# A two-layer encoder step on one core: first layer's 1/rms applied behind its projections, and a reordered recurrent branch

## The chip, the core and the metric

The kernel runs on one core of a Trainium2 chip. TensorE (PE) multiplies matrices into PSUM; VectorE (DVE), ScalarE (ACT) and GpSimd (POOL) do the elementwise work; SyncE (SP) issues all DMAs. The metric is the device time of one execution in microseconds (us), the median of a few executions. Times of single instructions, waits and clocks come from one profiled execution.

## What is computed

One inference step of a two-layer encoder, in fp32, for 1024 prompt frames and 64 sample frames (T = 1088 columns) of width 1024. Layer 0 (called AB in the kernel) feeds two attention groups from one projection; layer 1 (CD) feeds a forgetting attention C and a Griffin recurrent branch D. Around the change:

```python
def rmsnorm(x, g):
    y = x * lax.rsqrt(jnp.mean(x * x, axis=-1, keepdims=True) + EPS) * g

# each layer: x += W_out [mixer outputs](rmsnorm(x)); x += SwiGLU(rmsnorm(x))

def rg_lru(u, h0, w_a, b_a, w_x, b_x, lam):          # u: width-4 causal conv of dx
    r = sigmoid(blockdiag(u, w_a) + b_a)
    i = sigmoid(blockdiag(u, w_x) + b_x)
    log_a = -8.0 * r * softplus(-lam)
    a = exp(log_a)
    b = sqrt(-expm1(2.0 * log_a)) * (i * u)
    h = scan(a, b, h0)                                # h[t] = a[t] h[t-1] + b[t]
    # o_d = h * gelu(dg)
```

The projection of a normalized row is (x * g * 1/rms) W. Since 1/rms is one number per frame, it can be applied to x, or to the product (x * g) W.

## The kernel before, in words

Activations lie transposed: partitions are features (8 blocks k of 128), columns are frames, cut in three chunks `CH` of 384, 384 and 320 columns. Every fp32 matmul operand is split in a rounded high half and a remainder (`split`: ACT writes the high half, L235; DVE or POOL subtracts for the low half, L236), and a product takes three matmuls (high x high, high x low, low x high). A projection of one chunk by one weight block of 128 columns is therefore 8 x 3 = 24 matmuls (`gemm` L263 to L265; `gemm_steps` L275 where it is fed in slices between attention steps).

Layer AB consists of eight units, 0 to 7. A unit projects queries, keys and values (`proj`), unloads PSUM (`put_q`: ACT L351 and L352 write scaled high halves, DVE L356 the low halves; `new_k`: a DVE copy L369 to a staging tile, then `put_k` L332 to L335; `new_v`: DVE copy L379, PE transposes L385 and L388, then splits) and then computes scores (L487, L488), softmax and outputs, while the next unit's projections fill PE. Later units read the normalized halves `hh` and `hl` that unit 0 made.

`start` is unit 0. It loads x chunk 0 in eight pieces, then the query weights, then x chunk 1. `addsq` squares a piece on ACT (L300, L303) and adds on DVE (L304); `rms` averages by a matmul (L285) and takes 1/rms by Ln and Exp on ACT (L289 or L291, L292); `norm` multiplies x * g * r on DVE (L313) and splits the result. Chunk 0's norm comes first; its loop carries the squares of chunk 1. The key and value weights are loaded behind it. Then each chunk takes three projections; behind the query projection of a chunk stands the norm of the next one.

The order of each engine's instructions is laid out by a scheduler from data dependencies; `issue_after` keeps a named instruction ahead. Temporaries are rings: `tmp`, `stg` (staging, two slots), `nat`, `ot`; a ring's slot is reused when its last reader is done, a DMA that writes it out included. SP issues DMAs in order, and each waits for the one eight earlier.

At the head of layer CD, `recurrent` runs four blocks m = 0 to 3 of 128 features. For each it projects (`d_in`, `d_gate`: copy L1381), convolves on DVE (`d_conv` L1371, L1373), multiplies by the gate weights on PE (`d_gates` L1396 to L1398) with sigmoids on ACT (L1399) that free the PSUM banks, does gelu (`d_gelu`: ACT square L1355, POOL L1356, DVE L1357, ACT tanh L1360 and L1362, DVE L1363), and closes (`d_close`: POOL products L1411, ACT tanh L1413, exponentials and square roots L1418 to L1422, DVE scans L1425 and L1426). Between them `between` gives out six slices of C's first queries and keys. Sigmoid and tanh share one ACT table, the logarithm and exponential another; a change is a table load (L192). dx, u, G and R of a block are taken from a pool of eight slots and handed back by `d_close`, whose tile t overwrites u. DVE's forget-gate scans (L1306, L1307) stand between block 0 and 1.

## Time and profile before

| | us |
|---|---|
| median of 3 runs | 2711.04 |
| lowest, highest | 2710.79, 2717.03 |
| the profiled execution | 2712.83 |
| its span | 2711.0 |

The span of the profile is the time from the first to the last recorded instruction; the profiled execution's own time is 1.83 us more. A row of a timeline gives start, length, engine, line, operation, output<-input, and in brackets the idle time of the engine before it and what ended it. In the stretches (start:end, length, then busy time and number of instructions) a granted clock below 1.00 means that PE ran at a lower rate for part of the stretch. Of the page's parts, the busy times say which engine is the limit overall, the waits what PE stood still for, and the timeline where.

### The profile page before, as it was taken

The page shows a single profiled execution, that of the slowest core. Times are in us where ns is not written, and L with a number is a line of the kernel's source. Part 1 is how long each engine was busy: PE and PEld are TensorE (multiplying, and loading weights), DVE is VectorE, ACT ScalarE, POOL GpSimd, SP SyncE. Part 2 cuts the span into 40 slices and gives each one's busy share as a digit, 9 for nine tenths or more (in the row PEclk, how much of TensorE's full clock was granted, in tenths as well). Part 3 has the DMA queues.
Part 4 walks back from the last instruction along what each step waited for, and adds up shares of the span by engine and source line. Part 5 has one row for each costly group of instructions (what it writes and reads, how often), then busy time and mean ns, then how long its engine had stood idle before and what let it go on. Part 6 is the DMA issues. An engine that isn't in the chain of part 4 may idle for free. (4 is left out here: it accounts for less than half of the span.)

```text
span 2711.0 us, 44897 instructions
## 1 busy us (share of the span) xinstructions
PE 2596.9 (96%) x17610; PEld 2525.3 (93%) x17610; DVE 1325.7 (49%) x2763; ACT 1196.2 (44%) x2373; POOL 1155.1 (43%) x939
## 2 busy tenths in 40 slices
PE   6999999999999999999998979999999999999998
PEld 5899999889899999999998969988989999999998
DVE  7666666777432333422156557777743233242214
ACT  5666667764322233311135566686432323331112
POOL 5222222324666666422335433343366666641230
PEclk9999999999999999999999989999999999999999
DMA  6222222342222222442232342234322122244211
GB/s 204 73 71 69 78 63 62 104 151 92 83 95 66 81 72 87 141 154 72 74 105 60 52 80 79 78 123 150 100 86 97 64 82 70 88 141 153 72 55 67
DMA packets 115109, 250.21 MB, mean 92 GB/s; under 512 B 21432, under 2 KB 70848, under 8 KB 114896
## 3 DMA queue, kind: packets, MB, share of 16 engines
q1 hardware_dynamic: 114896, 247.33, 29.9%
q8 instruction: 138, 2.26, 0.4%
q14 instruction: 75, 0.61, 0.1%
HBM read 179.09 MB, written 65.43 MB: 90 GB/s over the span
## 5 line engine op out<-in xcount | busy, mean ns | idle before, releaser
L236 POOL TENSOR_TENSOR split_arena<-arena,split_arena 128x512 fp32r<-128x512 f32 (+5 forms) x501 | 756.7, 1522 | 1181.6 <-ACT split_arena L235 1091.7
L1070 PE MATMUL banks<-split_arena 128*128 128x272 f32 x7392 | 944.5, 290 | 23.3 <-ACT arena L1077 8.0
L1070 PEld LDWEIGHTS banks<-split_arena 128*128 128x128 f32 x7392 | 937.6, 190 | 30.0 <-ACT arena L1077 8.8
L235 ACT ACTIVATE split_arena<-arena 128x512 fp32r<-128x512 f32 (+10 forms) x664 | 458.8, 707 | 1020.3 <-PE banks L1070 291.9
L275 PE MATMUL banks<-split_arena 128*128 128x384 f32 (+1 forms) x3384 | 632.0, 333 | 3.4 <-POOL split_arena L236 2.3
L275 PEld LDWEIGHTS banks<-split_arena 128*128 128x128 f32 x3384 | 558.5, 189 | 10.9 <-POOL split_arena L236 2.9
L1182 PE MATMUL banks<-split_arena 128*128 128x384 f32 (+1 forms) x1056 | 345.1, 327 | 2.2 <-DVE arena L1148 1.4
L1184 PE MATMUL banks<-split_arena 128*128 128x384 f32 (+1 forms) x1056 | 344.4, 326 | 0.0
L1183 PE MATMUL banks<-split_arena 128*128 128x384 f32 (+1 forms) x1056 | 344.2, 326 | 0.0
L236 DVE TENSOR_TENSOR split_arena<-banks,split_arena 128x512 fp32r<-128x512 f32 (+4 forms) x312 | 167.4, 541 | 89.9 <-ACT split_arena L235 87.2
L499 DVE CUSTOM_DVE_ANT_0 arena<-banks,arena 128x384 f32<-128x384 f32 (+4 forms) x368 | 175.5, 493 | 56.4 <-PE banks L488 40.2
L1182 PEld LDWEIGHTS banks<-split_arena 128*128 128x128 f32 x1056 | 198.2, 188 | 3.6 <-DVE arena L1148 2.0
L1183 PEld LDWEIGHTS banks<-split_arena 128*128 128x128 f32 x1056 | 198.2, 188 | 0.3
L1184 PEld LDWEIGHTS banks<-split_arena 128*128 128x128 f32 x1056 | 198.2, 188 | 0.0
L235 ACT ACTIVATE split_arena<-banks 128x512 fp32r<-128x512 f32 (+4 forms) x312 | 146.7, 476 | 97.4 <-PE banks L604 43.3
L236 DVE TENSOR_TENSOR split_arena<-arena,split_arena 128x1088 fp32r<-128x1088 f32 (+8 forms) x163 | 154.0, 952 | 70.9 <-ACT split_arena L235 70.4
L1081 DVE TENSOR_TENSOR arena<-banks,arena 128x544 f32<-128x544 f32 (+1 forms) x46 | 32.2, 700 | 301.7 <-PE banks L1070 301.7
L501 ACT ACTIVATE arena<-arena 128x640 f32<-128x640 f32 (+8 forms) x216 | 156.3, 724 | 47.0 <-DVE arena L499 45.5
L1214 DVE TENSOR_TENSOR arena<-banks,arena 128x384 f32<-128x384 f32 (+1 forms) x96 | 51.1, 534 | 250.4 <-PE banks L1184 250.2
L604 PE MATMUL banks<-arena 128*128 128x128 f32 (+2 forms) x828 | 135.4, 276 | 18.8 <-DVE arena L520 11.5
L604 PEld LDWEIGHTS banks<-arena 128*128 128x128 f32 (+2 forms) x828 | 96.4, 141 | 37.7 <-DVE arena L520 15.1
L263 PE MATMUL banks<-split_arena 128*128 128x384 f32 (+1 forms) x312 | 106.7, 344 | 16.7 <-ACT arena L1399 10.0
(165 smaller groups left out, 3076.4 us busy)
## 6 DMA issues: line engine op xcount, KB each, us to landing
arena<-in_w_dram SPq DMA_DIRECT2D x120, 512.0 KB, 3.6
h_spill<-arena SPq DMA_DIRECT2D x22, 1088.0 KB, 4.2
arena<-h_spill SPq DMA_DIRECT2D x44, 544.0 KB, 4.4
arena<-in_abw_dram SPq DMA_DIRECT2D x24, 512.0 KB, 3.6
arena<-in_cdw_dram SPq DMA_DIRECT2D x20, 512.0 KB, 3.6
x_spill<-arena SPq DMA_DIRECT2D x48, 192.0 KB, 1.9
arena<-x_spill SPq DMA_DIRECT2D x16, 544.0 KB, 4.9
arena<-in_w_dram SPq DMA_DIRECT2D x19, 384.0 KB, 3.2
```

The source lines that it names most:

```text
L235: self.hi = self.nc.scalar.activation(hi, x, AF.Copy).ins
L236: lo = sub.tensor_tensor(lo, x, hi.bitcast(F32), op=ALU.subtract)
L263: nc.tensor.matmul(ps, wh[:, k], hh[k][:, c0:c0 + n], start=(k == ks[0]), stop=False)
L275: self.pe = self.nc.tensor.matmul(ps, x[:, k], y[k][:, c0:c0 + n], start=a and i == 0, stop=z and i == 2).ins
L499: nc.vector.tensor_tensor_reduce(o, p, t, -1.0, low, ALU.add, ALU.min, to)
L501: nc.scalar.activation(sb, sb, AF.Exp, bias=st[:, 0:1], scale=-1.0, accum_out=st[:, 1:2])
L604: nc.tensor.transpose(pt[:r, t * nq + s * m:t * nq + s * m + m], src, self.ident[:m, :m])
L1070: last = nc.tensor.matmul(bank[:, p], l[:, k], r[:, k, x], start=first and i == 0, stop=k == 3 and i == 2, skip_group_check=True)
L1182: nc.tensor.matmul(ps, wh, h[:, c0:c0 + n], start=j == j0, stop=False)
L1183: nc.tensor.matmul(ps, wh, lo[:, c0:c0 + n], start=False, stop=False)
L1184: nc.tensor.matmul(ps, wl, h[:, c0:c0 + n], start=False, stop=j == j1 - 1)
L1214: nc.vector.tensor_tensor(xs, pss[ci], xs, op=ALU.add)
```

## The change

Two independent parts. **First layer:** the high and low halves are made of x * g, without 1/rms. Query weights come first, then x chunk 0 in two halves of four pieces with the key weights between, then the value weights. The query and key projections of chunk 0 are each cut in two halves of k. The squares of a chunk stand behind its projections in the code, and 1/rms is kept in `self.rs` for all eight units and multiplied into the PSUM result: in place for queries, and as the unloading operation for keys and values. `norm` is not called by `start` any more; weights' low halves are made on DVE there. `layer_cd` sets `self.rs` to None.

**Recurrent branch:** the pool of slots is replaced by fixed places, with a place of its own for t; the tanh of gelu is held behind the sigmoids of the same block; the convolution of block m stands ahead of the closing of block m-1; the last slice of keys moves from the loop to behind the last gates.

```diff
+        self.rs = {c0: self.v(F_R + c0, n) for c0, n in CH}
...
     def put_q(self, d, c0, n, ps):
         nc = self.nc
+        if self.rs:
+            nc.vector.tensor_tensor(ps, ps, self.rs[c0], op=ALU.mult)
...
+    def unload(self, sg, c0, ps):
+
+        if self.rs:
+            self.nc.vector.tensor_tensor(sg, ps, self.rs[c0], op=ALU.mult)
+        else:
+            self.nc.vector.tensor_copy(sg, ps)
...
     def new_k(self, d, c0, n, ps, outs, keep, sub=None):
         sg = self.stg.get()[:, :n]
-        self.nc.vector.tensor_copy(sg, ps)
+        self.unload(sg, c0, ps)
+        if self.rs:
+            ps = sg
...
     def start(self, d, wq, wk, wv, pair, outs):
...
+        def parts(ci, ks=range(8)):
+
+            c0, n = CH[ci]
+            for k in ks:
+                x, g = self.x[k][ci], self.pcol(k)
+                hi, lo = self.hh[k][:, c0:c0 + n], self.hl[k][:, c0:c0 + n]
+                nc.scalar.activation(hi, x, AF.Copy, scale=g)
+                nc.vector.scalar_tensor_tensor(lo, x, g, hi.bitcast(F32), op0=ALU.mult, op1=ALU.subtract)
...
-        loadx(0)
-        w = [self.loadw(wq, rings)]
+        w = [self.loadw(wq, rings, sub=nc.vector)]
+        loadx(0, range(4))
+        parts(0, range(4))
+        w.append(self.loadw(wk, rings, sub=nc.vector))
+        loadx(0, range(4, 8))
+        parts(0, range(4, 8))
+        w.append(self.loadw(wv, rings, sub=nc.vector))
         loadx(1)
-        for k in range(8):
-            self.addsq(0, k, self.x[k][0])
-        last = self.norm(0, 0, 1, (nc.gpsimd, nc.gpsimd))
-        with self.tc.issue_after(last.ins):
-            w.append(self.loadw(wk, rings, sub=nc.vector))
-            w.append(self.loadw(wv, rings))
         loadx(2)
...
             p = [ring.get()[:, :n] for _ in range(3)]
-            for i in range(3):
+            if ci == 0:
+
+                for ks in (range(4), range(4, 8)):
+                    for i in range(2):
+                        for _ in self.gemm_steps(p[i], w[i], c0, n, ks=ks, first=ks[0] == 0, last=ks[0] == 4):
+                            pass
+            for i in range(2 if ci == 0 else 0, 3):
                 self.gemm(p[i], w[i], c0, n)
-                if i == 0 and ci < 2:
-                    self.norm(ci + 1, 0, 2 if ci == 0 else None)
+            for k in range(8):
+                self.addsq(ci, k, self.x[k][ci])
+            if ci < 2:
+                parts(ci + 1)
+            self.rms(ci, to=self.rs[c0], table=False)
             self.put_q(d, c0, n, p[0])
...
     def d_open(self, m, w=None):
-        b["slots"] = [self.D.get() for _ in range(3)]
-        for n, w, t in zip(("dx", "u", "G"), (T + 6, T + 6, T), b["slots"]):
-            b[n] = t[:, 0:w]
+        slot = lambda i, n: self.v(F_S + SLOT * i, n)
+        i, j, k, r = ((0, 1, 6, 4), (2, 3, 7, 4), (0, 1, 6, 7), (2, 3, 4, 1))[m]
+        b["dx"], b["u"], b["G"], b["R"], b["t"] = slot(i, T + 6), slot(j, T + 6), slot(k, T), slot(r, T), slot(5, T)
...
     def d_gelu(self, b, ci):
...
-        if ci == 0:
-            with self.tc.issue_after(self.table("sigmoid_and_others")):
-                nc.scalar.activation(z, z, AF.Tanh, scale=0.7978845608028654)
-        else:
-            nc.scalar.activation(z, z, AF.Tanh, scale=0.7978845608028654)
+        with self.tc.issue_after(b["gate"]):
+            b["tanh"] = nc.scalar.activation(z, z, AF.Tanh, scale=0.7978845608028654).ins
...
     def d_gates(self, b, m, after):
...
+        with contextlib.nullcontext() if self.closed is None else self.tc.issue_after(self.closed):
+            table = self.table("sigmoid_and_others")
...
-                nc.scalar.activation(dst[:, c0:c0 + n], ps, AF.Sigmoid, bias=self.dcol(bc, m))
+                with self.tc.issue_after(table):
+                    b["gate"] = nc.scalar.activation(dst[:, c0:c0 + n], ps, AF.Sigmoid, bias=self.dcol(bc, m)).ins
...
             self.d_gate(nb)
+            self.d_conv(nb, m)
             self.d_close(b, m - 1)
-            next(more)
-            self.d_conv(nb, m)
+            if m < 3:
+                next(more)
...
             self.d_gates(b, 3, b["pe"])
+            next(more)
             for ci in range(3):
                 self.d_gelu(b, ci)
```

How the order moves at three places. First ACT at the start of the program, before: L300 and L303 are the squares of x chunk 0, L235 128x1024 the high half of the query weights, L289 and L292 the Ln and Exp of 1/rms. (The brackets name the semaphores waited for: DMAHW is a load.)

```order
L300 ACTIVATE arena<-arena 128x384 [waits DMAHW1_49]
L303 ACTIVATE arena<-arena 128x384 [waits DMAHW2_49]
L303 ACTIVATE arena<-arena 128x384 [waits DMAHW3_49]
L303 ACTIVATE arena<-arena 128x384 [waits DMAHW4_49]
L303 ACTIVATE arena<-arena 128x384 [waits DMAHW5_49,DVE_49]
L303 ACTIVATE arena<-arena 128x384 [waits DMAHW6_49,DVE_49]
L303 ACTIVATE arena<-arena 128x384 [waits DMAHW7_49,DVE_49]
L303 ACTIVATE arena<-arena 128x384 [waits DMAHW0_49,DVE_49]
L192 ACT_TABLE_LOAD
L235 ACTIVATE split_arena<-arena 128x1024 [waits DMAHW1_49]
L300 ACTIVATE arena<-arena 128x384 [waits DMAHW2_49]
L289 ACTIVATE arena<-banks,arena 128x384 [waits PE_49]
```

The same place of the changed kernel, whose lines are its own: L224 128x1024 is the high half of weights, L449 that of x * g, L289 and L292 are now the squares.

```order
L224 ACTIVATE split_arena<-arena 128x1024 [waits DMAHW1_49]
L449 ACTIVATE split_arena<-arena 128x384 [waits DMAHW2_49]
L449 ACTIVATE split_arena<-arena 128x384 [waits DMAHW3_49]
L449 ACTIVATE split_arena<-arena 128x384 [waits DMAHW4_49]
L449 ACTIVATE split_arena<-arena 128x384 [waits DMAHW5_49]
L289 ACTIVATE arena<-arena 128x384
L292 ACTIVATE arena<-arena 128x384 x2
L224 ACTIVATE split_arena<-arena 128x1024 [waits DMAHW6_49]
L449 ACTIVATE split_arena<-arena 128x384 [waits DMAHW7_49]
```

The weights and the halves of x stand ahead of all squares. Further on, in the changed kernel, ACT comes to the last squares (L292 128x320) and the last 1/rms (L280, L281) in this order; L342 and L343 unload queries, L321 and L322 keys.

```order
L224 ACTIVATE split_arena<-arena 128x1024 [waits DMAHW7_49,PE_49]
L292 ACTIVATE arena<-arena 128x320 [waits DMAHW3_49,DVE_49]
L292 ACTIVATE arena<-arena 128x320 [waits DVE_49] x3
L280 ACTIVATE arena<-banks,arena 128x320 [waits PE_49]
L281 ACTIVATE arena<-arena 128x320 [waits Activation_49]
L342 ACTIVATE split_arena<-banks 64x320 [waits DVE_49]
L343 ACTIVATE split_arena<-banks 64x320
```

The first of these squares waits for a DMA, the one that writes chunk 1's new values out of a staging slot which overlaps the temporaries.

Second, ACT at the first block of the recurrent branch, before: L1355 is the square of gelu, L1360 and L1362 its tanh, L351 and L352 unload queries, L1399 are the sigmoids.

```order
L1355 ACTIVATE arena<-arena 128x384 [waits DVE_49]
L192 ACT_TABLE_LOAD
L1355 ACTIVATE arena<-arena 128x384 [waits Activation_49]
L1360 ACTIVATE arena<-arena 128x384 [waits DVE_49]
L351 ACTIVATE split_arena<-banks 64x384 [waits PE_49]
L352 ACTIVATE split_arena<-banks 64x384
L1399 ACTIVATE arena<-banks,arena 128x384 [waits PE_49] x2
```

In the changed kernel L1373 is that square, L342 and L343 unload queries, L181 is the table load, L1416 are the sigmoids, L1377 the tanh.

```order
L1373 ACTIVATE arena<-arena 128x384 [waits DVE_49]
L1373 ACTIVATE arena<-arena 128x384 [waits Activation_49]
L1373 ACTIVATE arena<-arena 128x320 [waits DVE_49]
L342 ACTIVATE split_arena<-banks 64x384 [waits PE_49]
L343 ACTIVATE split_arena<-banks 64x384
L181 ACT_TABLE_LOAD
L1416 ACTIVATE arena<-banks,arena 128x384 [waits PE_49] x2
```

The tanh moved behind the sigmoids, and the third square, which waits for DVE, ahead of them.

Third, PE at the gates of the last block, before: L1396 to L1398 are the gates' last matmuls, L487 and L488 the first scores of C, L275 the projection of values, L385 their transposes.

```order
L1396 MATMUL banks<-split_arena 128x320
L1397 MATMUL banks<-split_arena 128x320
L1398 MATMUL banks<-split_arena 128x320
L487 MATMUL banks<-split_arena 64x320
L488 MATMUL banks<-split_arena 64x320
L487 MATMUL banks<-split_arena 64x320
L275 MATMUL banks<-split_arena 128x384 x3
L275 MATMUL banks<-split_arena 128x320 x24
```

In the changed kernel L1412 to L1414 are the gates, L252 to L254 the last keys (20 of their 24 matmuls stand here, of which the first rows are shown).

```order
L1412 MATMUL banks<-split_arena 128x320
L1413 MATMUL banks<-split_arena 128x320
L1414 MATMUL banks<-split_arena 128x320
L253 MATMUL banks<-split_arena 128x320
L254 MATMUL banks<-split_arena 128x320
L252 MATMUL banks<-split_arena 128x320
```

The last keys moved from ahead of the gates to behind them; behind the 20 stand 35 matmuls of the value projection (L264) and then its first transposes (L385).

More of the change, by code (lines that the diff above doesn't have):

```diff
@@ L67 @@
 F_STG2 = 15808
+F_R = 14464
 GROUPS = [(12064 + 2176 * i, 544) for i in range(4)] + [(7360, 544), (38720, 544), (9536, 544), (4416, 544)] + \
@@ L115, in free @@
         del self.live[at]
-class Slots:
-    def __init__(self, ap, off, size, n):
-        self.all = [ap[:, off + size * i:off + size * (i + 1)] for i in range(n)]
-        self.free = list(self.all)
-    def get(self):
-        return self.free.pop(0)
-    def put(self, *slots):
-        self.free.extend(slots)
 class Blocks:
@@ L172, in __init__ @@
         self.tmp = self.tmp3
-        self.S, self.D = Heap(M, F_S, 6144), Slots(M, F_S, SLOT, 8)
+        self.S = Heap(M, F_S, 6144)
         self.stg, self.nat, self.ot = ring(F_STG, 384, 2), ring(F_NAT, 384, 2), ring(F_OT, 256, 2)
@@ L276, in gemm_steps, with rms @@
             yield "z", n * 1.25e-3
-    def rms(self, ci, parts=None, to=None):
+    def rms(self, ci, parts=None, to=None, table=True):
         nc = self.nc
@@ L286, in rms @@
         r = (self.rb.get() if to is None else to)[:, :n]
-        if ci == 0:
+        if ci == 0 and table:
             with self.tc.issue_after(self.table("natural_log_exp_and_others")):
@@ L378, in new_v @@
         sg = self.stg.get()[:, :n]
-        nc.vector.tensor_copy(sg, ps)
+        self.unload(sg, c0, ps)
         npr = min(n, TP - c0)
@@ L436, in start, with loadx @@
         ring = Ring(self.PS, [512 * i for i in range(5)], 512)
-        def loadx(ci):
+        def loadx(ci, ks=range(8)):
             c0, n = CH[ci]
-            for k in range(8):
+            for k in ks:
                 self.dma(self.x[k][ci], I["xT"][k * 128:k * 128 + 128, c0:c0 + n])
-        loadx(0)
-        w = [self.loadw(wq, rings)]
-        loadx(1)
-        for k in range(8):
-            self.addsq(0, k, self.x[k][0])
-        last = self.norm(0, 0, 1, (nc.gpsimd, nc.gpsimd))
-        with self.tc.issue_after(last.ins):
-            w.append(self.loadw(wk, rings, sub=nc.vector))
-            w.append(self.loadw(wv, rings))
+        def parts(ci, ks=range(8)):
+            c0, n = CH[ci]
+            for k in ks:
+                x, g = self.x[k][ci], self.pcol(k)
[9 more added lines that the diff above has]
+        w.append(self.loadw(wv, rings, sub=nc.vector))
+        loadx(1)
         loadx(2)
@@ L1405, in d_close @@
         c = self.rgc[:, m:m + 1]
-        t, a = u[:, 0:T], R
+        t, a = b["t"], R
         cuts = [slice(c0, c0 + n) for c0, n in CH]
@@ L1412, in d_close @@
         for x in cuts:
-            nc.scalar.activation(t[:, x], R[:, x], AF.Tanh, scale=c)
+            with self.tc.issue_after(b["tanh"]):
+                nc.scalar.activation(t[:, x], R[:, x], AF.Tanh, scale=c)
         table = self.table("natural_log_exp_and_others")
@@ L1421, in d_close @@
             nc.scalar.activation(t[:, x], t[:, x], AF.Ln, scale=-1.0)
-            nc.scalar.activation(t[:, x], t[:, x], AF.Exp, scale=0.5)
+            self.closed = nc.scalar.activation(t[:, x], t[:, x], AF.Exp, scale=0.5).ins
             nc.vector.tensor_tensor(Ig[:, x], Ig[:, x], t[:, x], op=ALU.mult)
@@ L1430, in d_close @@
         self.dma(self.oTd[4 + m], b["G"])
-        self.D.put(*b["slots"])
     def gate_weights(self):
@@ L1464, in recurrent @@
         self.gate_weights()
+        self.closed = None
         stg, self.stg2 = self.stg, Ring(self.M, [F_STG2], 384)
@@ L1516, in layer_cd @@
         self.lastu = 3
+        self.rs = None
         rest = self.recurrent(pending, self.qkv_views(0), W[0], W[4], I["cckT"][0], (O["c_kT"][0], O["sc_kT"][0]), 0)
```

5 lines of the change are left out of this document (1 added, 4 removed).

## The prediction

> **What bounds the kernel now.** I read the page first, then TensorE's (PE's) busy time by stretches, its waits, and its timeline where it waits.
>
> ```profile
> span 2711.0 us, 44897 instructions
> PE 2596.9 (96%) x17610; PEld 2525.3 (93%) x17610; DVE 1325.7 (49%) x2763; ACT 1196.2 (44%) x2373; POOL 1155.1 (43%) x939
> ```
>
> PE works 2596.9 of 2711.0 us. The change takes no matmul away, so it can win only PE's 114 us of idleness and the time PE runs at half rate. The stretches (start:end, length, PE busy, instructions, granted clock, DMA share, GB/s) say where those lie:
>
> ```profile
> 0.00:20.00 20.00, 4.16 (x8) 1.00 0.82 272
> 20.00:40.00 20.00, 17.07 (x75) 1.00 0.56 167
> 40.00:60.00 20.00, 16.32 (x80) 0.91 0.78 204
> 60.00:80.00 20.00, 16.59 (x89) 0.83 0.47 142
> 100.00:700.00 600.00, 579.88 (x3766) 550.65 (x3765) 408.31 (x1081) 390.40 (x867) 171.81 (x151) 0.99 0.27 82
> 1460.00:1480.00 20.00, 11.44 (x53) 0.74 0.39 113
> 1560.00:1580.00 20.00, 9.99 (x43) 0.74 0.42 14
> ```
>
> (In the 600 us row the busy times are PE, its weight loads, DVE, ACT, POOL.) Up to 80 us PE idles 25.9 us, two thirds of it in the first 20, where DMA is 82% busy. From 100 to 700 us it is 97% busy. In the recurrent section two stretches idle 8.6 and 10.0 us, at a clock of 0.74. PE's waits name the releasers (total, times, longest):
>
> ```profile
> PE banks L285 <- DVE arena L304: 12.8, 3, 11.1
> PE banks L263 <- ACT arena L1399: 10.0, 3, 8.6
> PE banks L487 <- POOL split_arena L334: 5.9, 1, 5.9
> PE banks L385 <- DVE arena L379: 5.8, 3, 3.7
> ```
>
> The first is the sum of squares ahead of the first projection; the second are the recurrent branch's sigmoids, which free PSUM banks; the third the last keys; the fourth transposes of values.
>
> **The start.** PE's own timeline (start, length; the bracket is the idle time before):
>
> ```profile
> 11.06 1.65 PE L285 MATMUL banks<-arena 128*128 128x384 f32 x2 [11.06 <-DVE arena L304]
> 16.82 0.69 PE L263 MATMUL banks<-split_arena 128*128 128x384 f32 x1 [4.11 <-ACT split_arena L235]
> 18.66 0.52 PE L265 MATMUL banks<-split_arena 128*128 128x384 f32 x1
> 18.98 0.52 PE L263 MATMUL banks<-split_arena 128*128 128x384 f32 x1
> 21.68 0.69 PE L264 MATMUL banks<-split_arena 128*128 128x384 f32 x1 [0.90 <-POOL split_arena L236]
> 26.94 0.34 PE L265 MATMUL banks<-split_arena 128*128 128x384 f32 x1
> 27.11 0.33 PE L263 MATMUL banks<-split_arena 128*128 128x384 f32 x1
> 74.04 0.31 PE L264 MATMUL banks<-split_arena 128*128 128x320 f32 x1
> 74.19 0.31 PE L265 MATMUL banks<-split_arena 128*128 128x320 f32 x1
> 76.53 0.33 PE L487 MATMUL banks<-split_arena 128*64 128x320 f32 x1 [2.03 <-issue]
> ```
>
> The first projection begins at 16.82, the first score at 76.53. Matmuls follow each other every 0.32 us at first (18.66 to 18.98), every 0.17 from about 27 on, every 0.15 when 320 wide. Three projections of three chunks are 72 matmuls a chunk: 144 x 0.173 + 72 x 0.147 = 35.5 us; with about 3.5 for the means (1.65 for the first two) and the transposes, 39. So 76.5 - 39 = 37.5 us before the first score are waits or half rate.
>
> What the pieces cost now:
>
> ```profile
> arena<-in_abw_dram SPq DMA_DIRECT2D x24, 512.0 KB, 3.6
> 11.72 1.06 ACT L235 ACTIVATE split_arena<-arena 128x1024 fp32r<-128x1024 f32 x1
> 21.97 1.21 DVE L236 TENSOR_TENSOR split_arena<-arena,split_arena 128x1024 fp32r<-128x1024 f32 x1
> 4.34 0.52 ACT L303 ACTIVATE arena<-arena 128x384 f32<-128x384 f32 x1
> 15.60 1.67 DVE L313 SCALAR_TENSOR_TENSOR arena<-arena 128x384 f32<-128x384 f32 x3
> 10.43 1.28 ACT L192 ACT_TABLE_LOAD   x1
> 16.84 4.79 POOL L236 TENSOR_TENSOR split_arena<-arena,split_arena 128x384 fp32r<-128x384 f32 x4 [1.58 <-ACT split_arena L235]
> 0.00:80.00 80.00, 45.17 (x93) 0.94 0.66 196
> ```
>
> After the change the query weights are issued first, at about 1.2: landed by 4.8 (3.6 us), high halves at 5.9 (ACT 1.06), then one high half of x (0.52). First matmul at about 6.6 instead of 16.8. Where it used to take a multiplication (DVE, 0.56), a rounding (ACT, 0.52) and a subtraction (POOL, 1.20) for each of 24 pieces of x, it takes the rounding and one DVE operation of 0.56. DVE then has 24 of these, 21 additions of the same size and three weight splits, 45 x 0.55 + 3 x 1.21 = 28 us by some 50: not the bound. PE's course: chunk 0 is 72 x 0.173 = 12.5, plus 4.0 for 27 matmuls at half rate (27 x 0.147), plus 1 for pieces that come late: done at about 24 (second half of x: 4 x 192 KB behind 1.8 MB, at 272 GB/s by 11 us, before PE has used the first). Chunk 1: 12.5 + 1.5, chunk 2: 10.6 + 1: done at 49.5.
>
> The sums of squares are late next. They no longer gate a projection, but each 1/rms gates unloading the chunk, and so the first score. ACT has 45.2 us of work in the first 80 (last row above, ACT alone) and about 43 still ahead of the first score; the squares share temporaries with the value copy and the cached keys, so two of them wait for value writes to land (192 KB, 2.8 us, behind 384 KB reads that take 6.6):
>
> ```profile
> rel_rows<-in_relrow_dram SPq DMA_DIRECT2D x8, 384.0 KB, 6.6
> out_a_vT_dram<-arena SPq DMA_DIRECT2D x2, 192.0 KB, 2.8
> ```
>
> I put the last 1/rms at 51.5 (50 to 58), and 5 us behind it, as now between copy, splits and score, the first score at 56.5 (54 to 62). By the new order 25 matmuls of the next unit (4.4 us) stand ahead of that score. So the waste is 56.5 - 39 - 4.4 = 13 instead of 37.5: a gain of 24. I take 22, since ACT at 43 of 56 us will be late somewhere; the range is 14 to 27.
>
> A rule speaks against this start. *TensorE: Matmul & The Clock Gate* of the Trainium skill (Part 1, HAM oscillation) says PE drops to half rate after an idle window of about 3.4 us, and that feeding it in pieces shorter than the waits keeps it there. The trace agrees after the 4.11 us wait (0.32 us a matmul until about 27); by the rule the sum above would hold only if the feed has no such gaps, and the third rival prices the contrary.
>
> **Multiplications by 1/rms.** Unit 0's nine are in the course above. Units 1 to 7 gain three each, 21 on DVE, in place in PSUM ahead of the query copy: as a 0.56 us operation each, 11.6 us. DVE is busy 68% from 100 to 700 us, PE 97%: they lie beside matmuls, and the copies of keys and values become multiplications of the same size. Their price is a bank freed 0.56 us later, against a chunk of 24 x 0.173 = 4.2 us: 0 to 3 us in all, I take 1. The table load that goes at the start (1.28 us of ACT) lies within the wait ahead of 16.82, which is counted whole above: 0 beyond it.
>
> **The recurrent section.**
>
> ```profile
> 1461.28 5.25 DVE L1306 TENSOR_TENSOR_SCAN arena<-arena 8x1024 f32<-8x1024 f32 x2 [2.39 <-DMA out_c_logfT_dram<-arena]
> 1469.73 1.01 DVE L1357 TENSOR_TENSOR arena<-arena 128x384 f32<-128x384 f32 x2
> 1472.38 0.69 PE L263 MATMUL banks<-split_arena 128*128 128x384 f32 x1 [8.56 <-ACT arena L1399]
> 1565.07 0.44 PE L1396 MATMUL banks<-split_arena 128*128 128x384 f32 x1 [3.27 <-ACT split_arena L235]
> 1566.33 0.69 PE L1397 MATMUL banks<-split_arena 128*128 128x384 f32 x1 [0.82 <-DVE split_arena L236]
> 1576.83 0.53 PE L487 MATMUL banks<-split_arena 128*64 128x320 f32 x1 [5.91 <-POOL split_arena L334]
> 1587.35 0.69 PE L385 MATMUL banks<-arena 128*128 128x128 f32 x2 [3.73 <-DVE arena L379]
> ```
>
> *First block, 8.56 us.* "Sigmoids ahead" does not cure it. In the new order all three gelu squares still precede the sigmoids on ACT, and the third needs a two-slot buffer that a DVE multiplication frees, which stands behind the forget-gate scans and two steps of the convolution (done 1469.7). The square then runs at about 1470.3, and the query copies and a table load of 1.28 before the sigmoids: the bank comes at 1473.6 instead of 1472.4, **1.2 us worse**.
>
> *Last block.* The convolution of m=3 goes ahead of the closing of m=2, so the gates' 3.27 + 0.82 and about 2 of half rate go (the clock of this stretch is 0.74): -6. The 20 matmuls left of the last keys and 24 of the values now stand behind the gates, in the 5.91 wait: -5.9. What is late next: the first transposes of values wait for a DVE copy behind the third gelu, at about 1578 to 1580, by which PE will have done 7 us of this work: 3 to 4 us come back, and another 1 to 2 at the out_c_vT buffer that DVE reaches earlier. Blocks two and three: 0 (the sigmoids' other two waits are 10.0 - 8.6 = 1.4 us together, and move either way). Sum 1.2 - 6 - 5.9 + 5 = **-6** (-9 to +1).
>
> **The sum.** -22 + 1 - 6 = -27, with the profiled execution's 2712.83 (span 2711.0 and 1.8 around it) 2685.8; it lies 1.8 above the median of 2711.04, so for the median 2711.0 - 27 = 2684.
>
> **Rivals.**
> 1. *The rms chain takes the gain.* Squares and 1/rms of chunk 2 come late (ACT's 43 us, value writes behind 384 KB reads): first score at 64 to 68. For it: ACT's load. Against: the squares have no other reader. The start gives 13 to 16, the rest as above or less: total -12 to -19, about 2696.
> 2. *Everything works.* First score at 53, DVE's copy no longer late: -27 and -9 to -11: about 2674.
> 3. *PE stays at half rate.* If waits for pieces of x, weights and DVE halves kept the first 216 matmuls slow, they cost 0.147 each for 189 more of them, 27.8 us: nothing is won, 2712. Against: the wait of 0.90 us at 21.68 did not keep PE from full rate by 27. This is what the page named above would expect of a starved start.
> 4. *Slower: the query multiplications hold banks.* A multiplication queued on DVE, in order, behind another unit's softmax holds its projection's bank. It decides once a chunk is held longer than the 4.2 us of matmuls that cover it by 1.7 us: 21 x 1.7 = 36 us against 27 won, 2720. For it: DVE at 68%. Against: keys and values already wait for such a DVE copy today, and from 100 to 700 us all waits of PE together are 3%.
> 5. *The start does not begin earlier*, because weights and x share DMA at 82% and land together: PE begins at 12, 5 us later than forecast, with the rest in step; -22 in all, inside the forecast's range.
>
> **The numbers.** The forecast (-20 to -33, rival 5 in it) 0.56; rival 1 (-9 to -20) 0.20; rival 2 (beyond -33) 0.14; rival 3 and its like, within 0.3% (8 us, about what a measurement of this kernel can tell from no change), 0.05; rival 4, 0.05. Faster 0.90. The range leaves out the ends of rivals 1 and 2 and both last ones: 2673 to 2698.
>
> **What would show it.** Right: first projection near 6.6, first score near 56, PE's first 80 us with 10 to 14 us less idle than 25.9 plus half-rate matmuls fewer; the 8.56 wait still there, near 9.8; the waits at 1565 and 1576 gone, one for the value copy left. Wrong: first score after 62 with ACT or a value write as releaser (rival 1); spacing of 0.32 beyond 20 us (rival 3); new waits of PE on the query multiplication between 100 and 1300 us (rival 4); a first block without a wait.

## The result, and the profile after

The change takes 2691.72 us (median of 4 runs, 2690.54 to 2694.74) against 2714.03 us for the kernel before beside it (four runs; the three with the median of 2711.04 are among them): a ratio of 0.9921, 95% interval 0.9907 to 0.9936, some 21 us (17 to 25). The same kernel, run again beside experiments on two later occasions, gave 0.9909 (0.9895 to 0.9922) and 0.9920 (0.9907 to 0.9934). The forecast was 27 us less, 2684, in a range of 2673 to 2698. The time lies 7.7 us above the forecast: the gain is 4.7 us smaller (22.3 by the medians), and the kernel before took 3 us more here than the 2711.04 that the forecast started from.

The page and PE's stretches of the change (start:end, length, PE busy, instructions, clock, DMA share, GB/s):

```profile
span 2690.5 us, 44858 instructions
PE 2592.6 (96%) x17610; PEld 2525.5 (94%) x17610; DVE 1320.8 (49%) x2781; ACT 1196.9 (44%) x2372; POOL 1133.1 (42%) x921
```

```profile
0.00:20.00 20.00, 12.51 (x56) 1.00 0.89 310
20.00:40.00 20.00, 20.00 (x118) 1.00 0.76 227
40.00:60.00 20.00, 14.60 (x83) 0.83 0.71 207
60.00:80.00 20.00, 19.88 (x120) 1.00 0.21 53
1440.00:1460.00 20.00, 9.90 (x51) 0.75 0.44 128
1520.00:1540.00 20.00, 15.83 (x80) 0.83 0.41 50
1560.00:1580.00 20.00, 14.30 (x73) 0.83 0.63 96
```

PE's busy time fell by 4 us (the count of matmuls is the same, and one at half rate counts longer), the span by 20.5. In the first 80 us PE idles 13.0 us where it idled 25.9. One stretch of the start is now bad (40 to 60), and the recurrent section has three. PE's largest waits:

```profile
PE banks L252 <- ACT arena L1416: 14.3, 2, 10.1
PE banks L385 <- DVE arena L354: 9.3, 2, 5.9
PE banks L274 <- DVE arena L293: 7.1, 3, 5.4
```

The sigmoids (L1416) head the list with more than before (10.0 then); the wait on the sum of squares (L293) is down from 12.8. The start on PE's, ACT's and DVE's timelines:

```profile
6.89 0.69 PE L264 MATMUL banks<-split_arena 128*128 128x384 f32 x1 [6.89 <-ACT split_arena L449]
...
22.81 0.81 PE L274 MATMUL banks<-arena 128*128 128x384 f32 x2
...
53.43 1.43 PE L274 MATMUL banks<-arena 128*128 128x320 f32 x2 [5.40 <-DVE arena L293]
54.19 4.52 PE L264 MATMUL banks<-split_arena 128*128 128x384 f32 x15
...
60.51 0.30 PE L504 MATMUL banks<-split_arena 128*64 128x320 f32 x1
```

```profile
47.67 0.47 ACT L292 ACTIVATE arena<-arena 128x320 f32<-128x320 f32 x1 [4.12 <-DMA out_a_vT_dram<-arena]
...
55.47 0.47 ACT L281 ACTIVATE arena<-arena 128x320 f32<-128x320 f32 x1
```

```profile
48.18 5.20 DVE L293 TENSOR_TENSOR arena<-arena 128x320 f32<-128x320 f32 x6 [6.07 <-ACT arena L292]
```

The first projection begins at 6.89 (forecast 6.6), chunk 0 is done at 22.8 (24), the first score comes at 60.5 (56.5, within 54 to 62). In between stands the wait that the forecast named: ACT stands 4.12 us until chunk 1's values are written out of the staging slot that its temporaries overlap, DVE adds late, PE waits 5.40 for the last mean, and 15 matmuls behind it take 4.52 us, about 0.3 each: half rate. The last 1/rms (L281) is ready at 55.9, 4.6 us ahead of the first score.

The recurrent section of the change, PE, then ACT and DVE:

```profile
1457.36 0.69 PE L252 MATMUL banks<-split_arena 128*128 128x384 f32 x1 [10.10 <-ACT arena L1416]
1533.28 0.69 PE L252 MATMUL banks<-split_arena 128*128 128x384 f32 x1 [4.17 <-ACT arena L1416]
1565.69 0.69 PE L385 MATMUL banks<-arena 128*128 128x128 f32 x2 [5.93 <-DVE arena L354]
```

```profile
1454.06 0.47 ACT L1373 ACTIVATE arena<-arena 128x320 f32<-128x320 f32 x1 [7.10 <-DVE arena L1375]
...
1527.92 0.47 ACT L1373 ACTIVATE arena<-arena 128x320 f32<-128x320 f32 x1 [4.40 <-DVE arena L1375]
```

```profile
1524.75 0.85 DVE L1386 TENSOR_SCALAR arena<-arena 128x1091 f32<-128x1091 f32 x1 [6.55 <-DMA arena<-in_dconvT_dram]
```

The third gelu square (L1373 128x320) waits 7.10 us for DVE, and six sigmoids wait behind it, as forecast. A second wait for sigmoids, of 4.17 us, was not forecast: in the third block the same square waits 4.40 us for DVE, and DVE for the input of the convolution (6.55, L1386).

Where the 20.5 us lie along the program is read from the first and last starts of lines that stand for places: unit 0's first outputs (L541, now L558), the feed-forward part (L1070, now L1087), the gates of the recurrent branch (L1396, now L1412) and the scores (L487, now L504). A row gives the shortest, median and longest duration in ns, then first and last start. Before, and then the change:

```profile
L541 PE MATMUL banks<-arena x40: 275/378/483, 96.9 to 322.6; 128*128 128x256 f32 x32, 128*128 128x64 f32 x8
L1070 PE MATMUL banks<-split_arena x7392: 282/288/595, 663.0 to 2436.9; 128*128 128x272 f32 x200
L1396 PE MATMUL banks<-split_arena x24: 306/337/522, 1460.7 to 1570.3; 128*128 128x384 f32 x16, 128*128 128x320 f32 x8
L487 PE MATMUL banks<-split_arena x312: 277/365/793, 76.5 to 1883.6; 128*128 128x384 f32 x68, 128*128 128x512 f32 x48, 128*128 128x256 f32 x28, 128*64 128x320 f32 x12
```

```profile
L558 PE MATMUL banks<-arena x40: 275/378/484, 76.4 to 302.1; 128*128 128x256 f32 x32, 128*128 128x64 f32 x8
L1087 PE MATMUL banks<-split_arena x7392: 282/288/596, 646.4 to 2416.3; 128*128 128x272 f32 x200
L1412 PE MATMUL banks<-split_arena x24: 306/336/338, 1444.1 to 1550.3; 128*128 128x384 f32 x16, 128*128 128x320 f32 x8
L504 PE MATMUL banks<-split_arena x312: 277/365/794, 60.5 to 1861.9; 128*128 128x384 f32 x68, 128*128 128x512 f32 x49, 128*128 128x256 f32 x27, 128*64 128x320 f32 x12
```

The lead is 20.5 us at unit 0's outputs, 16.6 at the feed-forward part and at the first gates, 21.7 at the last score. So the start won 20.5, units 0 to 7 lost 3.9, and the stretch from the first gate to the last score shrank from 422.9 to 417.8, by 5.1; the second feed-forward part gave 1.2 back. The same four places in the kernels that were run:

| kernel | lead at unit 0's outputs | lost in the units | first gate to last score |
|---|---|---|---|
| before | 0 | 0 | 422.9 |
| the change | 20.5 | 3.9 | 417.8 |
| the change, second and third profile | 21.3, 20.0 | 1.9, 0.9 | 416.1, 414.3 |
| first layer alone | 21.1 | 3.8 | 422.9 |
| recurrent part alone | 2.7 | -0.5 | 417.4 |
| no query multiplication in units 1 to 7 | 21.7 | -0.3 | 412.4 |
| squares in own temporaries | 22.4 | 1.1 | 418.6 |
| third square behind | 17.8 | 3.4 | 417.9 |
| third square and keys behind | 21.6 | 2.3 | 419.3 |
| all three | 21.9 | 2.5 | 417.7 |
| queries to SBUF | 19.2 | 12.3 | 415.6 |
| constants first | 19.8 | 0.7 | 417.6 |
| constants, temporaries, queries to SBUF | 21.6 | 14.4 | 418.1 |

Each row is one profiled execution (the change has three). Code that is the same comes out up to 4 us apart: the start of the change stands unaltered in seven of these profiles, and leads by 17.8 to 21.7; the recurrent part alone has the start of the kernel before and yet leads by 2.7. Differences below 4 us in one row are not read as effects. A profiled execution can also lie off its kernel's median: that of the recurrent part alone (2703.19 us) is the fastest of its five, median 2708.14, that of the third square (2692.19) the slowest of its four, median 2687.52.

### The profile page after: what moved, and what is told of

It is laid out like the page before. It is cut to its first block, busy times and chain, and to the rows that moved or that the text cites. A ratio compares the mean times of both kernels' runs of the same rounds, so it can differ in the third digit from the quotient of the medians.

```text
span 2690.5 us, 44858 instructions
## 1 busy us (share of the span) xinstructions
PE 2592.6 (96%) x17610; PEld 2525.5 (94%) x17610; DVE 1320.8 (49%) x2781; ACT 1196.9 (44%) x2372; POOL 1133.1 (42%) x921
## 4 chain that ended last, share of the span: by engine, by line
PE 76%; DVE 6%; ACT 5%; issue 5%; DMA 4%; POOL 3%; SPq 0%; DVEq 0%; ACTq 0%; POOLq 0%
PE banks L1087 32%; PE banks L264 14%; PE banks L1199 6%; PE banks L1201 6%; PE banks L1200 6%; PE banks L621 3%; ACT split_arena L224 2%; PE banks L504 2%; POOL split_arena L225 2%; PE banks L505 1%; PE banks L546 1%; PE banks L547 1%; DVE split_arena L225 1%; DMA arena<-o_spill 1%; ACT arena L518 1%
## 5 line engine op out<-in xcount | busy, mean ns | idle before, releaser
L225 POOL TENSOR_TENSOR split_arena<-arena,split_arena 128x512 fp32r<-128x512 f32 (+6 forms) x483 | 733.1, 1530 | 1171.3 <-ACT split_arena L224 1073.9
L1087 PE MATMUL banks<-split_arena 128*128 128x272 f32 x7392 | 946.3, 290 | 22.6 <-ACT arena L1094 7.1
L1087 PEld LDWEIGHTS banks<-split_arena 128*128 128x128 f32 x7392 | 939.2, 190 | 29.5 <-ACT arena L1094 8.0
L224 ACT ACTIVATE split_arena<-arena 128x512 fp32r<-128x512 f32 (+9 forms) x640 | 446.3, 715 | 1013.8 <-PE banks L1087 292.1
L264 PE MATMUL banks<-split_arena 128*128 128x384 f32 (+1 forms) x3432 | 648.8, 336 | 11.8 <-ACT split_arena L449 6.9
L264 PEld LDWEIGHTS banks<-split_arena 128*128 128x128 f32 x3432 | 572.7, 191 | 20.4 <-ACT split_arena L449 6.9
L1199 PE MATMUL banks<-split_arena 128*128 128x384 f32 (+1 forms) x1056 | 345.0, 327 | 2.8 <-DVE arena L1165 2.0
L1201 PE MATMUL banks<-split_arena 128*128 128x384 f32 (+1 forms) x1056 | 344.5, 326 | 0.0
L1200 PE MATMUL banks<-split_arena 128*128 128x384 f32 (+1 forms) x1056 | 344.2, 326 | 0.0
L224 ACT ACTIVATE split_arena<-banks 128x512 fp32r<-128x512 f32 (+4 forms) x312 | 147.1, 477 | 102.1 <-PE banks L621 48.4
L621 PE MATMUL banks<-arena 128*128 128x128 f32 (+2 forms) x828 | 134.6, 273 | 12.8 <-DVE arena L537 7.9
L621 PEld LDWEIGHTS banks<-arena 128*128 128x128 f32 (+2 forms) x828 | 95.7, 140 | 31.4 <-DVE arena L537 11.2
L504 PE MATMUL banks<-split_arena 128*128 128x256 f32 (+3 forms) x312 | 113.2, 365 | 0.0
```

The source lines that it names most:

```text
L224: self.hi = self.nc.scalar.activation(hi, x, AF.Copy).ins
L225: lo = sub.tensor_tensor(lo, x, hi.bitcast(F32), op=ALU.subtract)
L264: self.pe = self.nc.tensor.matmul(ps, x[:, k], y[k][:, c0:c0 + n], start=a and i == 0, stop=z and i == 2).ins
L504: nc.tensor.matmul(ps[:, :mw], qd[:, q0:q0 + m], kk[:, k0 + s:k0 + s + mw], start=True, stop=False)
L621: nc.tensor.transpose(pt[:r, t * nq + s * m:t * nq + s * m + m], src, self.ident[:m, :m])
L1087: last = nc.tensor.matmul(bank[:, p], l[:, k], r[:, k, x], start=first and i == 0, stop=k == 3 and i == 2, skip_group_check=True)
```

## The experiments

Two halves of the change come first, then each suspected wait. Each ratio is to the kernel before on the same chip; that kernel took 2717.85 us beside the first layer alone, the recurrent part alone, the squares in own temporaries and the third square, and 2712.33 to 2714.03 beside all others.

**The first layer alone**: the kernel before, with `start`, `put_q`, `unload` and `rs` of the change, and its own recurrent branch.

> The first layer's part of the change alone, recurrent branch as before. Reading of the traces: first score 16 us earlier with 25 matmuls already done, 20.5 us ahead by unit 0's values, about 4 us of it lost again in units 4 to 7, so 16 to 17 us ahead at the recurrent section and at the end: ratio to before about 0.994; the sigmoids' wait of 8.6 us as before. Rival (the loss in the units comes with the recurrent part's other code, not with this one): 20 to 21 us ahead at the end, ratio 0.9925.

Measured: ratio 0.9922 (0.9910 to 0.9935). Lead 21.1, lost 3.8, recurrent stretch 422.9 as before. PE's waits in the recurrent section are those of the kernel before:

```profile
PE banks L266 <- ACT arena L1430: 10.4, 3, 8.7
```

The profile sides with the theory: the loss in the units is there without the recurrent part's code, and the span is 16.6 us shorter than that of the kernel before. The ratio sides with the rival's 0.9925: it stands for 21.7 us, and the theory's 0.994 lies outside its interval. The places compare with a profile from another chip, the ratio with the 2717.85 us of this one; which of the two is nearer for the end of the program stays open.

**The recurrent part alone**: the kernel before, with `d_open`, `d_gelu`, `d_gates`, `d_close` and `recurrent` of the change.

> The recurrent part alone, first layer as before. Reading of the traces: the first block's wait for sigmoids grows from 8.6 to about 10, the third's from 0.8 to about 4, the waits ahead of the last gates and of the last keys go, a wait for a copy of values of about 6 comes: net 4 to 5 us faster, ratio about 0.998. Rival (the waits only change places, and the 4 us are chance alignment with the first part): no difference, 0.9995 to 1.0005.

Measured: ratio 0.9963 (0.9951 to 0.9976), 7 to 13 us faster. By places, the stretch shrank by 5.5, the first block's wait grew as expected:

```profile
PE banks L249 <- ACT arena L1385: 14.9, 2, 9.9
```

The rival falls: the part gains by itself. But the theory's 0.998 lies outside the interval too: the 10 us of the ratio are more than the 5.5 of the stretch. In the profile, 2.7 us of the 9.6 stand at unit 0's outputs and 2.8 more come between there and the first gates, where nearly all code is that of the kernel before; the rest is not settled. The gains of the two halves by ratio (21.7 and 9.7 us) add up to 31.4, more than the whole change gave elsewhere (21 to 25); the whole did not run on this chip.

**No query multiplication in units 1 to 7.** Queries of those units stay without their 1/rms.

```diff
...
-        if self.rs:
+        if self.rs and self.first:
             nc.vector.tensor_tensor(ps, ps, self.rs[c0], op=ALU.mult)
...
```

> The changed kernel without the in-place multiplications of queries by 1/rms in units 1 to 7: 21 DVE operations of 0.55 us less (those queries stay without their factor, keys and values keep theirs). Theory (the lead of 20.5 us after unit 0 shrinks to 16.6 by the end of the units because each multiplication keeps a projection's bank and DVE's queue longer): the lead at the start of the feed-forward part stays within 1.5 us of that behind unit 0, 2 to 4 us faster than the change. Rival (the loss is waits on softmax and a spell of half rate that fall as they fall): the same 3 to 4 us are lost, no difference from the change.

Measured: ratio 0.9902 (0.9887 to 0.9917), the change beside it 0.9909. The lead grew from 21.7 to 22.0, instead of shrinking by 0.7 to 3.9 us, as in the nine profiles that keep the multiplication in place (2.3 on average). In the recurrent part alone, which has no such multiplication either, it grew by 0.5. This points to the multiplications, for 2.3 + 0.3 = 2.6 us; but it is one profile, the difference is less than equal code shows, and the ratios show none. The loss is likely theirs, not shown to be.

**Queries to SBUF**: the product goes to a tile of its own, so the bank is free after one operation.

```diff
         if self.rs:
-            nc.vector.tensor_tensor(ps, ps, self.rs[c0], op=ALU.mult)
+            sg = self.v(F_R + T, n)
+            nc.vector.tensor_tensor(sg, ps, self.rs[c0], op=ALU.mult)
+            ps = sg
```

> The changed kernel with the queries' multiplication by 1/rms written to a tile in SBUF instead of in place, so that a projection's bank is free after one DVE operation, before ACT and DVE have read it again. Without the 21 multiplications the lead over the kernel before grew by 0.5 us between unit 0's values and the feed-forward part; with them it shrank by 1 to 4. Theory (the price is the bank held longer): it shrinks by less than 1.5 us here, 1 to 3 us faster than the change. Rival (the price is DVE's time in its queue, where softmax waits): it shrinks as in the change, no difference.

Measured: ratio 0.9948 (0.9935 to 0.9961), the change beside it 0.9920: slower than the change by about 8 us, 12.3 lost in the units. (All 24 query multiplications move here, unit 0's three too.) Neither theory foresaw this. What the trace shows is that the low halves (L349), which now read two operands of SBUF, take up to 2.11 us, where from PSUM they never took over 0.56 (min/median/max in ns):

```profile
L349 DVE SCALAR_TENSOR_TENSOR split_arena<-arena,split_arena x48: 473/555/2114, 27.2 to 477.2; 64x384 fp32r<-64x384 f32 x32, 64x320 fp32r<-64x320 f32 x16
L349 DVE SCALAR_TENSOR_TENSOR split_arena<-banks,split_arena x24: 482/546/562, 1465.6 to 1752.8; 64x384 fp32r<-64x384 f32 x16, 64x320 fp32r<-64x320 f32 x8
```

The 48 of the first row are busy for 35.0 us, where the same 48 of the change (in its third profile) take 25.6. Four of the longest (near 141, 206, 340 and 475 us) each ran beside a split of weights on POOL. The longest begins at 339.53 and ends at 341.64; POOL's operation ends at 341.29:

```profile
338.90 2.39 POOL L225 TENSOR_TENSOR split_arena<-arena,split_arena 128x1024 fp32r<-128x1024 f32 x1 [7.47 <-ACT split_arena L224]
```

The Trainium skill, *SBUF - State Buffer* (SBUF: two separate sides), says that a DVE operation with two SBUF inputs and a GpSimd operation that reads SBUF lock each other out for a whole instruction; the trace agrees with 2114 against 562 ns, and with the end of the long operation just behind POOL's. Whether these 9.4 us of DVE or the single tile, which all units now share, carry the 8 us was not tried. So the run does not decide between its two theories: whether the price of the multiplication in place is the held bank or DVE's time in its queue stays open.

**Squares in temporaries of their own** (x chunk 0's place, free by then):

```diff
...
+            if ci:
+                self.sq = Ring(self.M, [F_X[0] + 384 * i for i in range(4)], 384)
...
+        self.sq = None
```

> The changed kernel, with the squares of x chunks 1 and 2 in four temporaries of their own (in x chunk 0's place, which is free by then) in place of the three shared with the value staging and the cached keys. Theory (the last squares wait for the write of chunk 1's values to land): ACT's wait of 4.1 us for that write goes, PE's 5.4 us ahead of the last mean falls below 1, and the half rate behind it goes; first score at 54 to 55 instead of 60.5, 5 to 6 us faster than the change, about 2686. Rival (ACT's and DVE's own load sets the last 1/rms, whatever the temporaries): PE still waits over 3 us there, gain below 2 us.

Measured: ratio 0.9898 (0.9884 to 0.9913), without the change on the same chip. ACT's wait for the write and PE's 5.40 are gone, but the first score comes at 58.6:

```profile
41.57 0.55 PE L385 MATMUL banks<-arena 128*128 128x128 f32 x3 [2.01 <-DVE arena L352]
51.12 0.70 PE L274 MATMUL banks<-arena 128*128 128x320 f32 x2
...
58.57 0.33 PE L507 MATMUL banks<-split_arena 128*64 128x320 f32 x1 [2.13 <-DMA split_arena<-split_arena]
```

```profile
40.04 0.56 DVE L340 TENSOR_TENSOR banks<-banks,arena 128x384 f32<-128x384 f32 x1
```

The cause of the wait is shown, its worth was overrated. DVE now adds chunk 2's squares ahead of chunk 1's unloading, which begins at 40.04 (L340) instead of 38.31; PE waits 2.01 us for the value copy, 13 matmuls behind it run 0.27 us apart instead of 0.15, and the last projection ends at 51.1 instead of 48.0. Behind the last 1/rms a 2.13 us wait for the copy of query halves between partitions appears. Of 5 to 6 us 1.9 remain in this profile. The two other kernels with these temporaries have their first score at 57.8 and 57.5, and nine profiles without them lie between 58.7 and 63.2, mean 60.5: by all of these the move is worth 2 to 3 us.

**The third gelu square behind the sigmoids:**

```diff
-        nc.scalar.activation(z2, ps, AF.Square)
+        with self.tc.issue_after(b["gate"]) if ci == 2 else contextlib.nullcontext():
+            nc.scalar.activation(z2, ps, AF.Square)
```

> The changed kernel, with the third gelu square of a block held behind that block's sigmoids. Theory (the third square, which waits for a staging slot that DVE frees behind the forget-gate scans, holds up the sigmoids): the first block's wait falls from 10.1 to 3 or 4 us, the third block's from 4.2 to below 2, with less half rate behind them: 7 to 10 us faster than the change, about 2683. Rival (the sigmoids are held by the query copies, the table load or the branch's own buffers): the wait stays above 8, gain below 2 us.

Measured: ratio 0.9887 (0.9872 to 0.9902), without the change on the same chip. The first block's wait falls to 2.05, as the theory says. But the third block's grows to 9.86; ACT and DVE there:

```profile
1449.07 0.44 PE L252 MATMUL banks<-split_arena 128*128 128x384 f32 x1 [2.05 <-ACT arena L1417]
```

```profile
1531.52 0.69 PE L252 MATMUL banks<-split_arena 128*128 128x384 f32 x1 [9.86 <-ACT arena L1417]
```

```profile
1528.57 0.48 ACT L321 ACTIVATE split_arena<-banks 64x384 fp32r<-64x384 f32 x1 [8.51 <-DVE arena L354]
```

```profile
1527.98 0.56 DVE L354 COPY arena<-banks 128x384 f32<-128x384 f32 x1 [2.35 <-DMA out_c_kT_dram<-arena]
```

The sigmoids stand on ACT behind key halves (L321), these behind a DVE copy (L354), that behind the convolution's wait for its input (6.48 us, L1387) and the write of the keys before (2.35). The stretch is 417.9: by the profile nothing of the 8 us is left. The ratio, the lowest of all, does not say so: its interval ends below 0.9907, where that of the change begins in two of its three measurements. The profile is of the slowest run of four, and the kernel before was slower on this chip, so that a real gain of some us is not excluded.

**That, and the second slice of keys behind the third block's gates:**

```diff
-            next(more)
+            if m < 3:
+                next(more)
             self.d_gates(b, m - 1, nb["pe"])
+            if m == 3:
+                next(more)
```

> The changed kernel with the third gelu square behind the sigmoids, and the second slice of keys (in the third block) moved behind that block's gates. Theory (with the square out of the way, the third block's sigmoids stand on ACT behind key halves that wait for a DVE copy, and that for the write of the keys before): the 9.9 us wait that the square's move left in the third block falls below 3, the first stays at 2: 12 to 14 us less waiting of PE in the two blocks than in the change; of it up to 3 us return at the last copies of values, 9 to 12 us faster than the change. Rival (DVE, waiting for the input of the third block's convolution, holds the branch whatever stands ahead of the sigmoids): the wait moves to the next gates or the values' transposes, gain over the change below 4 us.

Measured: ratio 0.9923 (0.9911 to 0.9936), the change beside it 0.9909: no gain. The rival holds. The waits for sigmoids shrink to 1.7, 2.0 and 0.3, and others come up in the third and the last block, for the copies that free banks ahead of the gates (L1364, and L1397 with 3.30 us), for values (L385, 3.76), and for PE's first transposes of softmax weights in C's attention (L621):

```profile
1517.07 0.69 PE L1413 MATMUL banks<-split_arena 128*128 128x384 f32 x1 [4.07 <-ACT arena L1364]
...
1594.36 0.46 PE L621 MATMUL banks<-arena 128*128 128x128 f32 x1 [4.41 <-DVE arena L537]
```

The stretch is 419.3. All kernels with this branch, in three arrangements of its waits, lie between 412 and 419, and the arrangement of the change alone between 412 and 418.6. No arrangement stands out. That PE waits for one chain of elementwise steps wherever the wait is put fits this; the chain itself was not measured.

**All three moves:**

> Both moves of the recurrent branch, and the squares of the first layer in temporaries of their own. If the three are independent: first score at 58 to 59 instead of 60.5 or later, 5 us less waiting at the start, 12 in the recurrent section; 13 to 17 us faster than the change, ratio to before about 0.986. If the waits are given back: above 0.989.

Measured: 0.9906 (0.9893 to 0.9920) against 0.9909: they are given back. The first score comes at 57.8.

**Constants first**: 12 matmuls of constants while PE waits for operands.

```diff
+        warm = self.mm.get()[:, :128]
+        for _ in range(12):
+            nc.tensor.matmul(warm, self.o1024, self.zero, start=True, stop=True)
```

> The changed kernel with 12 matmuls of constants (128x128, result not used) ahead of the first projection, while PE waits for its first operands. Theory (PE's half rate over the first 25 or so projection matmuls follows from its idleness until 6.9 us): they run 0.17 us apart from the first on or within a few, chunk 0's projections end 3 to 4 us earlier; of it 0 to 2 us reach the first score, since the last 1/rms waits for the write of values and not for PE. Rival (half rate comes from the gaps of operands that arrive one by one): the spacing stays 0.32 until about 15 us, no difference.

Measured: 0.9913 (0.9900 to 0.9925) against 0.9920, no difference. PE and its granted clock (the column 0.99, 0.50, 0.65, 1.00):

```profile
1.34 4.47 PE L437 MATMUL banks<-arena 128*128 128x128 f32 x24 [1.34 <-DVE arena L191]
6.85 0.45 PE L264 MATMUL banks<-split_arena 128*128 128x384 f32 x1 [1.04 <-ACT split_arena L452]
8.14 4.18 PE L264 MATMUL banks<-split_arena 128*128 128x384 f32 x14 [0.83 <-DVE split_arena L453]
```

```profile
6.00:8.00 2.00, 0.45 (x1) 0.99 1.01 352
8.00:10.00 2.00, 1.86 (x6) 0.50 1.07 403
10.00:12.00 2.00, 2.00 (x10) 0.65 1.02 388
12.00:14.00 2.00, 1.74 (x10) 1.00 1.04 353
```

The first projection matmul takes 0.45 instead of 0.69 us: PE was at full rate. Waits of 1.04 and 0.83 us around that one matmul then put it back to half, and chunk 0's first two projections are done no earlier (18.4 against 18.7). (The 12 matmuls are 24 in the trace.) The rival holds in the main: the feed sets the pace, though the spacing is back at 0.18 from 12.6 us on (33 matmuls in 5.99), not 15.

**Constants, own temporaries and queries to SBUF together:**

> The changed kernel with the squares' own temporaries, the constants ahead of the first projection, and the queries' multiplication into SBUF. With the squares freed of the write, PE's earlier end of the three chunks reaches the first score: 55 to 56 instead of 60; 5 to 8 us faster than the change, ratio to before 0.988 to 0.9895. If the pieces do not add, it is no better than the squares' temporaries alone, above 0.990.

Measured: 0.9954 (0.9941 to 0.9966). First score at 57.5, not 55 to 56, then 14.4 us lost in the units, as in the run with queries to SBUF alone.

**The change itself**, beside the runs of the second and the third occasion:

> The changed kernel once more, on the chip of the three beside it, so that they are compared with it and not only with the kernel before. Ratio to before 0.9907 to 0.9936 as measured; its first score between 58 and 63 us, since the same code's start has come out up to 3 us apart.

> The changed kernel beside the three, on their chip: ratio to before 0.991 to 0.9925.

Measured 0.9909 and 0.9920; first scores at 59.7 and 61.0. No kernel was faster than the change beside it by more than the intervals allow. The two with lower ratios, the squares' temporaries and the third square, ran without it on their chip. In plain times (2689.99 and 2687.52 us) they lie by the change's 2688.72 to 2691.72; whether they are faster stays open.

## Why the prediction was right, step by step

- *The start, -22*: measured -20.5 (-21.3 and -20.0 in the other profiles). The operands' arrival, PE's earlier begin and the three chunks were right within 2 us, chunk 2 being done at 48.0 for 49.5. The last 1/rms is ready at 55.9 where 51.5 was put, late by the chain that was named (squares that wait for a value write) and within the 50 to 58 that were allowed for it. From it to the first score are 4.6 us, where 5 were put. The half rate behind the 5.40 us wait is a second price of such idleness that the sum left out. Here it cost the first score some 1 us at most: the copies of query halves between partitions were issued until 57.6 and take 2.0 us to land, so that their last bytes came at about 59.6, and the score at 60.5.
- *The rule that spoke against the start*: the trace before shows half rate behind the 4.11 us wait, but no fall to it. The two matmuls at 11.06, ahead of that wait, take 1.65 us, and their like in the change, at 22.81, take 0.81: PE had been at half rate already. A fall stands behind the 5.40 us wait of the change.
- *The multiplications, +1 (0 to 3)*: perhaps mis-sized. The lead shrinks by 2.3 us on average where they are, in single profiles by up to 3.9, and grows by 0.3 and 0.5 where they are not. "A bank freed 0.56 us later" was not shown to be the mechanism, nor was another.
- *The first block, +1.2*: the wait grew by 1.5 (8.56 to 10.10; 9.42 and 9.6 in the other profiles), by the chain that was named: moving the square behind the sigmoids took 8 us of it away.
- *Blocks two and three, 0*: wrong. The third block's wait is 4.17 (2.5 in the other two profiles) where two waits had 1.4 together. The step that failed is that they "move either way": the rule seen in the first block, a third square behind DVE, was not carried to the third, where DVE waits for the convolution's input. Nor is the square all there: with it out of the way the wait was 9.86, behind key halves.
- *The last block*: the waits at 1565 and 1576 are gone, as forecast, and the values' copy holds PE for 5.93 and 3.34 us, where 3 to 4 and 1 to 2 were put: 4 us more.
- *Recurrent section, -6*: -5.1 to -8.6 in three profiles. That the sum is right is in part luck. PE's waits of which it is made (sigmoids, gates, last keys, values) are 23.7 us together before and 23.8 in the change (21 in its other profiles). What fell is a wait that the prediction does not name: PE's transposes of softmax weights in C's attention (L604, now L621) wait 9.8 us in the stretch before and 4.8 in the change, for DVE and ACT; another 1.7 us are PE's busy time. It goes with this part: 4.7 us with the recurrent part alone, 9.5 with the first layer alone. The largest row of this wait before, and then its like in the change:

```profile
PE banks L604 <- DVE arena L520: 4.9, 4, 3.5
```

```profile
PE banks L621 <- DVE arena L537: 1.2, 3, 0.4
```

- *The sum, -27*: the profile's -20.5 is -20.5 for the start, +3.9, -5.1, and +1.2 in the second feed-forward part, where the code is the same. All three terms came out on the side of less gain in this profile, and the range took it in.
- *Rivals*: the late rms chain is real, its wait of 4.12 seen and removed, but cost 2 to 3 us and not 8. Half rate throughout did not come: some 15 matmuls of chunk 0 were slow (6.89 to 12 us) where 27 had been allowed for, and it was done at 22.8, not 24. The slower side, queries that hold banks, was not seen; with queries to SBUF 8 us were given back, but there the bank is free after one operation.

## What to carry to other kernels

A linear scale can be moved behind a product when the product waits for it: the product can begin as soon as the first operands have landed. Price what reads the scale next, and the storage that its steps share with writes. Compare the length of a section from its first to its last instruction, and not only PE's list of waits: the two waits for sigmoids of 10.1 and 9.9 us were brought to 2 or less here and the section stayed as long.

## What the runs showed of the hardware

- PE at full rate fell back to half after two waits of 1.04 and 0.83 us with one matmul between them. *TensorE: Matmul & The Clock Gate* of the Trainium skill (Part 1, The HAM clock gate) speaks of an idle window of about 3.4 us; here a nearly idle stretch of 2.3 us (5.8 to 8.1) was enough. Behind a single wait of 2.01 us ahead of the value transposes it fell in the kernel with own temporaries (granted clock 0.70 from 44 to 48 us), and behind the same wait of 2.01 us it did not in the one with all three moves (1.00), so that the length of the wait alone does not decide.
- The granted clock stands at 1.00 in the first stretches of the change although six matmuls fill 1.82 us there, 0.3 each (the row below). Half rate at the very start shows in the spacing alone; with constants ahead, the same stretch reads 0.50.
- One and the same start came out up to 4 us apart between executions (17.8 to 21.7 us of lead).

The stretch of the change that the second point speaks of:

```profile
8.00:10.00 2.00, 1.82 (x6) 1.00 1.05 396
```

Its fourth column is the clock that the trace gives.
